# An input projection reordered: rows normalised first, gate tiles in pairs of seven chained products, attention last

## The chip, the cores and the metric

The kernel runs on one core of a Trainium2 chip. The metric is the device time of one launch in microseconds (us). The engines are named as in the profile: PE multiplies matrices (PEld loads its stationary operand), DVE is the vector engine, ACT the scalar engine, POOL the third elementwise engine, and SP issues the DMAs.

## The reference, cut to what matters

One encoder layer is applied to 512 prompt rows and 1024 sample rows (two sequences, same weights), with 1024 features, all in fp32:

```python
h = rms_norm(x, norm1_g)                       # per row
z = h @ w_in                                   # 1024 -> 6400 columns, 50 tiles of 128
#   conv value, conv gate (512) | pool (256) | short conv gb, gc, xv (768) | q, k, v (768) | gates (4 x 1024)
br_a = silu(layer_norm(depthwise31(a_val * sigmoid(a_gate)) + b)) @ w_out_a
br_b = pooled_means(z_pool) @ w_out_b
br_c = (gb * depthwise3(gc * xv)) @ w_out_c
br_d = neighbourhood_attention(q * 64**-0.5, k, v, rpb) @ w_out_d      # 4 heads of 64
merged = sum_i sigmoid(gate_i + b_i) * br_i
x = x + merged @ w_o
x = x + conv_glu_ffn(rms_norm(x, norm2_g))     # w_up 1024 -> 5632, depthwise3, silu, w_down 2816 -> 1024
return rms_norm(x, final_g)
```

## The kernel before

Everything is kept transposed: features on the 128 partitions, rows along the free axis, in three chunks of 512 rows (chunk 0 is the prompt, chunks 1 and 2 the sample). To keep fp32 accuracy each operand is split into a rounded high part and a low remainder, and each product is three matmuls (`mm3`, L112 to L115): high by high, high by low, low by high. One output tile of the input projection (128 of the 6400 columns) takes 3 chunks x 8 k-tiles x 3 = 72 matmuls of 512 columns. The order of the instructions on each engine is fixed at compile time by the framework's scheduler, which takes the earliest instruction of the program that it holds ready; on the chip each engine then works its queue in that order.

**Start.** The rows are split as they come, multiplied by the norm's gain alone (`split_x`, L109, L110). The two first gate tiles (PSUM tiles `zs`) follow the loads. The sums of squares are made beside them (`stats`), and the reciprocal root of the mean is broadcast to all partitions by a matmul with ones (`rms_scale`, `spread`) and kept in SBUF as `rb1`. Since the rows are not normalised, each tile that leaves PSUM is multiplied by `rb1` (`gate_evac`, L310).

**Plan.** The other 48 tiles stand in a list. After each tile `pump` emits background work up to a budget of 7.0:

```python
attention_pair(0); run_gates(9); drain()
conv_branch(0); run_gates(2); conv_branch(1); run_gates(9); drain()
then(conv_norm); attention_pair(1); run_gates(G3); drain()
pool_branch(0); run_gates(1); pool_branch(1); run_gates(1); drain()
short_branch(0); short_branch(1); run_gates(32)
```

An attention step (24 in all, a head pair by a block of 128 queries, cost 5.0) gathers its window of v on POOL (`vw`, L473), transposes it on PE (`vt`, L478) and splits it; then come scores, softmax, transposes of the probabilities (`tp`) and the product with v (`o`, L524 to L526). The 31 taps of each conv half run over 1552 columns on DVE (L579).

**Later stages.** A stage with eight PSUM tiles multiplies the branches by `w_out` (`y`), weighs them with the gates read back from DRAM and adds (`m`). Then `w_o` follows (`o`, L113 to L115), the second norm and the up projection. There 22 pairs of w_up tiles are each computed as two prompt tiles (24 matmuls each) and, for chunks 1 and 2, seven products of half-size blocks (12 matmuls each) in place of eight, in Winograd's form of Strassen's scheme. The sums of the weight blocks (`S1` to `S4`) are made on POOL, and the sums of the products on ACT and DVE. Last the down projection (`yp`) and the final norm.

Of the kernel before, what the change touches and what calls it, by code (L numbers as in the profile page):

```python
# [12 lines left out]
F32 = mybir.dt.float32  # L13
# [27 lines left out]
BUDGET = 7.0  # L41
# [3 lines left out]
SC_AT, EV_AT = 5, 15  # L45
ST = 3
G3 = 8
# [14 lines left out]
def encoder(ctx, tc, xT, w_in, w_out, w_o, w_up, w_dn, par, rrel, outT):  # L62
# [3 lines left out]
    def dram(name, shape):  # L66
        return tc.dram_tile(shape, F32, name=name)
# [8 lines left out]
    f_d = [dram(f"f_d{j}", [P, T]) for j in range(NJ)]  # L76
    late_d = {(n, k): dram(f"late_d{n}{k}", [P, C]) for n in LATE for k in range(4)}
# [34 lines left out]
    def mm3(ps, w, ws, x, first, last):  # L112
        PE.matmul(ps, w[0][:, ws], x[0], start=first, stop=False)  # L113
        PE.matmul(ps, w[0][:, ws], x[1], start=False, stop=False)  # L114
        PE.matmul(ps, w[1][:, ws], x[0], start=False, stop=last)  # L115
# [61 lines left out]
    with ExitStack() as outer:  # L177
# [42 lines left out]
        class UpWeights:  # L220
            def __init__(self):
                self.q = {}
# [5 lines left out]
            def parts(self, j):  # L228
                a = {}
                for n, f in (("1", NJ + j), ("2", j)):  # L230
                    raw = wp.tile([P, DM], F32, tag="wraw", name=f"wr_u{f}")
                    SP.dma_start(raw, w_up[f])
                    a[n + "1"], a[n + "2"] = raw[:, :C], raw[:, C:]
                w = self.q[j] = {}

                def plain(n):
                    w[n] = hl(f"A{n}h{j}"), hl(f"A{n}l{j}")
                    split(*w[n], a[n])

                def combo(n, tag, x, y, op):  # L240
                    t = self.stp.tile([P, C], F32, tag="st", name=f"S{n}_{j}")
                    G.tensor_tensor(t, x, y, op)
                    return t

                def mixed(n, tag, t):
                    o = wp.tile([P, DM], F32R, tag=tag, name=f"S{n}s{j}")
# [20 lines left out]
        wq = UpWeights()  # L267
# [10 lines left out]
        open_zps(4)  # L278

        def prompt(j, n):  # L280
            z = ztile(f"pp{n}{j}")
# [4 lines left out]
        def product(z, w, xn):  # L286
            for k in range(4):
                mm3(z, w, cols(k), ops[xn, k], k == 0, k == 3)
            return z

        with ExitStack() as mixer:
            bigp = pool(mixer, "bigp", 9)
# [7 lines left out]
            br = {}  # L300
            with ExitStack() as p1:
                sps = pool(p1, "sps1", 2, space=PSUM)
                mps = pool(p1, "mps1", 2, space=PSUM)
                gop = pool(p1, "gop", 3)
                rb1 = gop.tile([P, T], F32, tag="rb", name="rb1", bufs=1)

                def gate_evac(i, d):
                    def evac(c, z):
                        o = gop.tile([P, C], F32, tag="go", name=f"go{i}{d}{c}")
                        V.tensor_tensor(o, z, rb1[:, ch(c)], ALU.mult)  # L310
                        S.activation(o, o, AF.Sigmoid, bias=pc("bg", i * 8 + d))  # L311
                        SP.dma_start(gate_d[d][:, c, i, :], o)

                    return evac

                def gate_idx(i, d):
                    return 18 + 8 * i + d

                gates = [(i, d) for d in range(8) for i in range(4)]

                h = [[None] * KT for _ in range(NC)]
                with ExitStack() as p0:
                    np0 = pool(p0, "np0", 2)
                    xk = [big(f"x{k}") for k in range(KT)]
                    first = [load_w(w_in[gate_idx(*gates[n])], f"s{n}", None, (P, C)) for n in range(2)]

                    def load_x(k, c):
                        SP.dma_start(xk[k][:, ch(c)], xT[k * P : (k + 1) * P, ch(c)])

                    def split_x(k, c):  # L330
# [885 lines left out]
```

## Time and profile before

| | |
|---|---|
| time, median of 3 runs | 2269.69 us (2267.65 to 2270.16) |
| span of the profiled execution, first to last instruction | 2265.9 us |
| the three times stand above that span by | 1.8 to 4.3 us; the profiled execution's own time is not listed apart |
| PE busy | 2231.1 us, 9986 matmuls |
| DVE, ACT, POOL busy | 1339.6, 720.9, 545.9 us |
| moved by DMA | 195.63 MB |

Matmuls are pipelined: a recorded duration reaches over the start of the next, so the pace is read from start to start.

### The profile page before, as it was taken

What the parts mean: (1) busy time and instruction counts of PE and PEld (TensorE: products, weight loads), DVE (VectorE), ACT (ScalarE), POOL (GpSimd) and SP (SyncE); (2) the same over time, 40 slices, a digit from 0 to 9 for tenths busy, and PEclk for the clock granted to TensorE, in tenths of its full rate; (3) what the DMA queues carried; (4) which work ended last, traced back from release to release, by engine and by line L of the source; (5) the groups of instructions that cost most, each with busy time, mean ns of one, the idle gap of its engine ahead of it and who ended that gap; (6) DMA issues with size and microseconds to landing.
All of it is one profiled execution on the core that took longest, in us unless ns stands there. A gap on an engine that the chain in (4) does not pass through costs nothing.

```text
span 2265.9 us, 26328 instructions
## 1 busy us (share of the span) xinstructions
PE 2231.1 (98%) x9986; PEld 1817.6 (80%) x9986; DVE 1339.6 (59%) x1923; ACT 720.9 (32%) x1139; POOL 545.9 (24%) x671
## 2 busy tenths in 40 slices
PE   7999999999999999999998999999999999999997
PEld 5877888888777878888786788888888888888886
DVE  7345439932445442778339997777888876341414
ACT  6256411222156410302223543333333334221112
POOL 5023101000023101254234453344444430000001
PEclk9999999999999999999999999999999999999999
DMA  4211211222111110374432321111221225532231
GB/s 165 75 57 61 70 56 52 79 79 70 42 67 55 42 66 28 116 247 176 135 126 97 112 74 66 61 57 61 66 66 56 66 66 183 161 119 58 79 91 50
DMA packets 78351, 195.63 MB, mean 86 GB/s; under 512 B 8592, under 2 KB 11152, under 8 KB 75152
## 3 DMA queue, kind: packets, MB, share of 16 engines
q1 hardware_dynamic: 78224, 193.94, 25.6%
q8 instruction: 79, 1.29, 0.2%
q14 instruction: 48, 0.39, 0.1%
HBM read 135.71 MB, written 58.20 MB: 86 GB/s over the span
## 4 chain that ended last, share of the span: by engine, by line
PE 49%; DVE 2%; issue 0%; POOL 0%; ACT 0%; POOLq 0%; ACTq 0%
PE yp L113 5%; PE yp L114 5%; PE yp L115 5%; PE pp L114 3%; PE pp L115 3%; PE pp L113 3%; PE o L114 2%; PE o L113 2%; PE o L115 2%; PE p3T L115 1%; PE p3T L114 1%; PE p3T L113 1%; PE p1T L114 1%; PE p1T L115 1%; PE p1T L113 1%; PE p22T L115 1%
## 5 line engine op out<-in xcount | busy, mean ns | idle before, releaser
L113 PE MATMUL z<-hh,wh_i 128*128 128x512 f32 x1080 | 427.1, 395 | 0.0
L115 PE MATMUL z<-hh,wl_i 128*128 128x512 f32 x1080 | 423.6, 392 | 0.0
L114 PE MATMUL z<-hl,wh_i 128*128 128x512 f32 x1080 | 422.0, 391 | 0.0
L113 PEld LDWEIGHTS z<-hh,wh_i 128*128 128x128 f32 x1080 | 202.8, 188 | 46.4 <-issue 4.8
L115 PEld LDWEIGHTS z<-hh,wl_i 128*128 128x128 f32 x1080 | 202.8, 188 | 41.9 <-issue 0.7
L114 PEld LDWEIGHTS z<-hl,wh_i 128*128 128x128 f32 x1080 | 202.9, 188 | 40.9 <-issue 1.5
L113 PE MATMUL yp<-fs,wdhi 128*128 128x512 f32 x480 | 187.0, 391 | 0.0
L114 PE MATMUL yp<-fs,wdhi 128*128 128x512 f32 x480 | 186.9, 389 | 0.0
L115 PE MATMUL yp<-fs,wdlo 128*128 128x512 f32 x480 | 186.8, 389 | 0.0
L310 DVE TENSOR_TENSOR go<-z,rb 128x512 f32<-128x512 f32 x90 | 62.1, 690 | 193.2 <-PE z L115 193.2
L106 DVE TENSOR_TENSOR fs<-fr,fs 128x512 fp32r<-128x512 f32 x63 | 43.4, 691 | 182.1 <-ACT fs L105 182.1
L987 POOL TENSOR_TENSOR u<-u,u 128x512 f32<-128x512 f32 x63 | 97.6, 1549 | 193.5 <-DVE u L980 135.9
L311 ACT ACTIVATE go<-go,pt 128x512 f32<-128x512 f32 x96 | 69.4, 724 | 184.9 <-DVE go L310 180.0
L105 ACT CAST wh_i<-wr_i 128x1024 fp32r<-128x1024 f32 x44 | 46.3, 1052 | 241.9 <-PE z L114 224.4
L579 DVE SCALAR_TENSOR_TENSOR acc<-glu,pt,acc 128x1552 f32<-128x1552 f32 x60 | 112.7, 1879 | 1.6 <-ACT acc L577 0.4
L113 PEld LDWEIGHTS yp<-fs,wdhi 128*128 128x128 f32 x480 | 90.1, 188 | 19.3 <-issue 0.5
L114 PEld LDWEIGHTS yp<-fs,wdhi 128*128 128x128 f32 x480 | 90.1, 188 | 19.2 <-issue 0.5
L115 PEld LDWEIGHTS yp<-fs,wdlo 128*128 128x128 f32 x480 | 90.1, 188 | 18.9
L105 ACT CAST fs<-fr 128x512 fp32r<-128x512 f32 x63 | 39.1, 622 | 200.6 <-DMA fr<-f_d 98.7
L980 DVE SCALAR_TENSOR_TENSOR u<-c,pt,u 128x512 f32<-128x512 f32 x88 | 100.4, 1179 | 0.0
L1080 POOL TENSOR_TENSOR x<-x,rs 128x256 f32<-128x256 f32 x11 | 7.6, 731 | 366.1 <-DVE acc L1068 362.4
L979 DVE SCALAR_TENSOR_TENSOR u<-c,pt,u 128x512 f32<-128x512 f32 x88 | 86.9, 1025 | 0.0
(353 smaller groups left out, 4998.3 us busy)
## 6 DMA issues: line engine op xcount, KB each, us to landing
gate_d<-go SPq DMA_DIRECT2D x96, 256.0 KB, 2.0
g<-gate_d SPq DMA_DIRECT2D x24, 1024.0 KB, 4.9
wr_i<-in_w_in SPq DMA_DIRECT2D x45, 512.0 KB, 3.5
wr_u<-in_w_up SPq DMA_DIRECT2D x44, 512.0 KB, 3.5
f_d<-u SPq DMA_DIRECT2D x66, 256.0 KB, 2.0
fr<-f_d SPq DMA_DIRECT2D x66, 256.0 KB, 2.7
wdr<-in_w_dn SPq DMA_DIRECT2D x23, 512.0 KB, 3.7
x<-in_xT SPq DMA_DIRECT2D x24, 256.0 KB, 5.4
```

The costliest lines, as they stand in the source:

```text
L105: S.copy(hi, src)
L106: V.tensor_tensor(lo, src, hi.bitcast(F32), ALU.subtract)
L113: PE.matmul(ps, w[0][:, ws], x[0], start=first, stop=False)
L114: PE.matmul(ps, w[0][:, ws], x[1], start=False, stop=False)
L115: PE.matmul(ps, w[1][:, ws], x[0], start=False, stop=last)
L310: V.tensor_tensor(o, z, rb1[:, ch(c)], ALU.mult)
L311: S.activation(o, o, AF.Sigmoid, bias=pc("bg", i * 8 + d))
L579: V.scalar_tensor_tensor(a, g, w, a, ALU.mult, ALU.add)
L979: V.scalar_tensor_tensor(b, r[:, 0:C], pc("fc", f * 3), b, ALU.mult, ALU.add)
L980: V.scalar_tensor_tensor(b, r[:, 2 : C + 2], pc("fc", f * 3 + 2), b, ALU.mult, ALU.add)
L987: (V if j == NJ - 1 else G).tensor_tensor(uv, uv, ug, ALU.mult)
L1080: G.tensor_tensor(x, x, rs[:, :n], ALU.mult)
```

## The change

1. The rows of a chunk are normalised before they are split (`normalise`). So the first matmul needs the sum of squares over all eight k-tiles of chunk 0. No tile is multiplied by `rb1` on its way out. The first tiles are q0, q1 and k0 together.
2. q and k are written to DRAM in split form (`qk_d`). v is computed with the rows as stationary operand and 256 columns moving (`value_tile`), which gives it with rows on the partitions, and is written to DRAM once for each of four column blocks (`vt_d`). An attention step loads its v window in split form (`vv`); the gather, the transposes and the split of v are gone. The softmax's scaling by `ri` goes from DVE to ACT.
3. The two conv gates and values are computed early, their product is written to DRAM (`glu_d`), the taps run beside the gates in five steps per pair, and their result is written out as well (`acc_d`).
4. Thirty of the 32 gate tiles are computed as 15 pairs: the prompt chunk as before, chunks 1 and 2 by seven block products. Partial sums stay in PSUM: a product goes on adding to the tile of an earlier one after ACT or DVE has read it (`chain`).
5. Four normalised tiles that these pairs consume are read back and split again. Then a plan of 10 plain tiles follows (pool, short conv, two gates), with the 24 attention steps of cost 1.0 and a budget of 3.0 per tile, and the conv branch's layer norm beside the last two tiles.

```diff
-BUDGET = 7.0
+STEPS = 3.0
+TAPS = 5
+TPN = 34
-SC_AT, EV_AT = 5, 15
+SC_AT = 4
-G3 = 8
...
+    qk_d = {(n, p, x): dram(f"{n}{x}_d{p}", [P, T]) for n in "qk" for p in range(2) for x in "hl"}
+    vt_d = dram("vt_d", [4, T // GW, 32, 4 * P])
+    glu_d = [dram(f"glu_d{i}", [P, T]) for i in range(2)]
+    acc_d = [dram(f"acc_d{i}", [P, HI - LO]) for i in range(2)]
+    b12_d = [dram(f"b12_d{k}", [P, C]) for k in range(4)]
...
-        def product(z, w, xn):
+        def product(z, w, xn, first=True, chain=False):
             for k in range(4):
-                mm3(z, w, cols(k), ops[xn, k], k == 0, k == 3)
+                mm3(z, w, cols(k), ops[xn, k], first and k == 0, k == 3, chain)
             return z
...
+            def stats(c):
+                acc = tt(f"acc0_{c}")
+                for k in range(KT):
+                    if k == 0:
+                        S.activation(acc, x[k, c], AF.Square)
+                        continue
+                    q = tt(f"sq0_{c}{k}")
+                    S.activation(q, x[k, c], AF.Square)
+                    (G if c else V).tensor_tensor(acc, acc, q, ALU.add)
...
+            def normalise(k, c):
+                V.scalar_tensor_tensor(x[k, c], x[k, c], pc("g1", k), stat[c], ALU.mult, ALU.mult)
+                h[c][k] = hl(f"hh{k}_{c}"), hl(f"hl{k}_{c}")
+                split(*h[c][k], x[k, c])
+                if c == 2 and k < 4:
+                    SP.dma_start(b12_d[k], x[k, c])
...
+            stats(0)
+            scale(0)
+            for a in range(2):
+                split(*k0w[a], kraw[:, a * C : (a + 1) * C])
+            for c in range(NC):
+                zz = [ztile(f"zt{c}{n}") for n in range(3)]
+                if c + 1 < NC:
+                    stats(c + 1)
+                for k in range(KT):
+                    normalise(k, c)
+                    for n in range(3):
+                        w, ws = trio_w(n, k)
+                        mm3(zz[n], w, ws, h[c][k], k == 0, k == KT - 1)
+                    if k == SC_AT and c + 1 < NC:
+                        scale(c + 1)
+                for n in range(3):
+                    qk_out(*(("q", 0), ("q", 1), ("k", 0))[n], c, zz[n])
...
+            def value_tile(c, b):
+                z = ztile(f"zv{c}{b}")[:, :256]
+                for k in range(KT):
+                    xh, xl = (y[:, cols(b)] for y in h[c][k])
+                    wh, wl = (vw[m][k // 2][:, (k % 2) * 256 : (k % 2) * 256 + 256] for m in range(2))
+                    PE.matmul(z, xh, wh, start=(k == 0), stop=False)
+                    PE.matmul(z, xh, wl, start=False, stop=False)
+                    PE.matmul(z, xl, wh, start=False, stop=(k == KT - 1))
...
+            pairs = [(gates[2 * n], gates[2 * n + 1]) for n in range(15)]
+            wg = PairWeights("g", lambda n: tuple(w_in[gate_idx(*g)] for g in pairs[n]), tt)
+            wg.prepare(0)
+            for n, (ga, gb) in enumerate(pairs):
+                w = wg.q[n]
+                y, wz, xz = (ztile(f"{m}g{n}") for m in "ywx")
+                product(y, w["11"], "B11", True, True)
+                a = go(f"ga{n}")
+                S.copy(a, y)
+                if n + 1 < len(pairs):
+                    wg.prepare(n + 1)
+                z = prompt(n, "1", wg)
+                gate_out(*ga, 0, z, go(f"gp{n}"))
+                product(y, w["2"], "T2", False, True)
+                u2 = go(f"gu{n}")
+                S.copy(u2, y)
+                next(tap, None)
+                product(wz, w["3"], "T3", True, True)
+                p7 = go(f"gs{n}")
+                S.copy(p7, wz)
+                next(tap, None)
+                product(xz, w["12"], "B21")
+                V.tensor_tensor(a, xz, a, ALU.add)
+                gate_out(*ga, 1, a, a)
+                product(y, w["1"], "T1", False, True)
+                V.tensor_tensor(p7, y, p7, ALU.add)
+                gate_out(*gb, 2, p7, p7)
+                next(tap, None)
+                z = prompt(n, "2", wg)
+                gate_out(*gb, 0, z, go(f"gq{n}"))
+                next(tap, None)
+                product(wz, w["22"], "T4", False, True)
+                V.tensor_tensor(u2, wz, u2, ALU.add)
+                gate_out(*gb, 1, u2, u2)
+                product(y, w["4"], "B22", False, True)
+                gate_out(*ga, 2, y, go(f"gr{n}"))
...
-                        vw = ap.tile([P, 384], F32, tag="vw", name=f"vw{nm}", bufs=1)
...
-                        for i in range(nt):
-                            PE.transpose(vtp[:, cols(i)], vw[:, cols(i)], ident)
...
+                        vv = ap.tile([P, 3, 2 * P], F32R, tag="vv", name=f"vv{nm}")
+                        SP.dma_start(vv[:, :nt].bitcast(F32), vt_d[...])
...
-                            V.tensor_scalar(sv, sv, ri, None, ALU.mult)
+                            S.activation(sv, sv, AF.Copy, scale=ri)
...
                     def start():
-                        t["ot"] = br[3, p] = big(f"ot{p}")
+                        for n in "qk":
+                            for m in "hl":
+                                pl_, tag = (bigp, "big") if n == "q" else (kp, "k")
+                                t[n + m] = pl_.tile([P, PADW], F32R, tag=tag, name=f"{n}{m}{p}")
+                                SP.dma_start(t[n + m][:, :T].bitcast(F32), qk_d[n, p, m])
...
                 attention_pair(0)
-                run_gates(9)
+                pool_branch(0)
+                pool_branch(1)
+                sc = [short_head(0)]
                 drain()
...
+                attention_pair(1)
+                sc.append(short_head(1))
+                for g in gates[2 * len(pairs) :]:
+                    plain_gate(*g)
                 drain()
                 then(conv_norm)
+                for i in range(2):
+                    short_tail(i, sc[i])
                 drain()
```

## Rows read from the trace of the kernel before

**Rows 1.** The page: span, and busy time by engine.

```profile
span 2265.9 us, 26328 instructions
PE 2231.1 (98%) x9986; PEld 1817.6 (80%) x9986; DVE 1339.6 (59%) x1923; ACT 720.9 (32%) x1139; POOL 545.9 (24%) x671
```

**Rows 2.** PE's waits, longest first: total us, times, longest us.

```profile
PE rb L145 <- DVE dg L137: 5.7, 3, 2.7
PE zs L113 <- ACT hh L109: 5.3, 1, 5.3
```

**Rows 3.** Windows: start, 18 up-projection pairs, attention. Busy us (instructions) by engine.

```profile
0.00:60.00 60.00, 47.06 (x181) 33.46 (x182) 48.07 (x63) 37.95 (x62) 32.56 (x25) 0.97 0.45 160
1270.31:1810.67 540.36, 540.36 (x2378) 446.05 (x2377) 448.96 (x538) 204.19 (x333) 239.91 (x354) 1.00 0.19 63
10.00:20.00 10.00, 8.17 (x30) 5.44 (x29) 9.65 (x8) 9.62 (x18) 8.41 (x6) 1.00 1.05 397
```

**Rows 4.** PE in order of time: first matmuls, plain tile, attention.

```profile
7.10 0.63 PE L113 MATMUL zs<-hh,wh_s 128*128 128x512 f32 x1
7.53 0.63 PE L114 MATMUL zs<-hl,wh_s 128*128 128x512 f32 x1
...
208.74 0.28 PE L526 MATMUL o<-ph,vl 128*128 128x256 f32 x1
...
209.45 0.28 PE L526 MATMUL o<-ph,vl 128*128 128x256 f32 x1
...
215.72 0.49 PE L478 MATMUL vt<-pt,vw 128*128 128x128 f32 x3
216.15 0.45 PE L489 MATMUL s<-kh,qh 64*128 64x384 f32 x2
...
216.88 0.50 PE L113 MATMUL z<-hh,wh_i 128*128 128x512 f32 x1
...
224.15 0.44 PE L489 MATMUL s<-kh,qh 64*128 64x384 f32 x1
```

**Rows 5.** Groups by line and shape: count, busy us, mean ns of one.

```profile
L525 PEld LDWEIGHTS o<-pl,vh 128*128 128x128 f32 x64 | 12.1, 188 | 3.2 <-issue 1.3 <-DVE pl L106 1.2
L110 DVE SCALAR_TENSOR_TENSOR hl<-x,pg,hh 128x512 fp32r<-128x512 f32 x24 | 30.0, 1286 | 5.8 <-ACT hh L109 5.8
L856 DVE SCALAR_TENSOR_TENSOR x<-x,pg,rb 128x512 f32<-128x512 f32 x16 | 10.9, 740 | 0.3 <-PE rb L145 0.3
L992 ACT COPY a<-p11B 128x512 f32<-128x512 f32 x20 | 11.3, 567 | 0.0
L371 ACT ACTIVATE sq<-x 128x512 f32<-128x512 f32 x21 | 13.1, 623 | 3.7 <-POOL acc L372 3.6
L579 DVE SCALAR_TENSOR_TENSOR acc<-glu,pt,acc 128x1552 f32<-128x1552 f32 x60 | 112.7, 1879 | 1.6 <-ACT acc L577 0.4
```

**Rows 6.** DVE and PE in order of time: one reciprocal root and its broadcast.

```profile
2015.40 0.94 PE L132 MATMUL rb<-ones,acc 128*128 128x1 f32 x8
...
2016.38 0.16 DVE L135 TENSOR_SCALAR rs_v<-rb 128x4 f32<-128x4 f32 x1 [2.21 <-PE rb L132]
...
2018.55 0.69 DVE L137 TENSOR_TENSOR acc<-pt,rs_y 128x512 f32<-128x512 f32 x1
...
2019.30 1.13 PE L145 MATMUL rb<-acc,ones 128*128 128x512 f32 x2
```

**Rows 7.** SP and ACT at the start: a load's issue, its reader.

```profile
1.66 0.42 SPq L328 DMA_DIRECT2D x<-in_xT  x1
...
4.53 0.72 ACT L109 ACTIVATE hh<-x,pg 128x512 fp32r<-128x512 f32 x1 [1.07 <-DMA x<-in_xT]
```

**Rows 8.** ACT in order of time within one attention step.

```profile
217.89 1.28 ACT L511 ACT_TABLE_LOAD   x1
...
222.79 0.99 ACT L105 CAST ph<-tp 128x384 fp32r<-128x384 f32 x2 [1.97 <-PE tp L517]
```

**Rows 9.** DMA issues: count, KB each, median us from issue to landing.

```profile
g<-gate_d SPq DMA_DIRECT2D x24, 1024.0 KB, 4.9
```

## What the change does to the time, forecast from these rows

> **What bounds the kernel now.** I read the page first. PE is busy for 2231 of 2266 us [rows 1], but a matmul's record overlaps the next, so that alone proves little. The list of PE's waits is the test: its longest entries are 5.7 and 5.3 us in total, both around the first and second norm [rows 2]. PE therefore sets the end nearly everywhere, and a removed matmul is worth its start-to-start pace. That pace comes from a long undisturbed stretch: 2378 matmuls in 540.36 us [rows 3], 0.227 us each for 512 columns. Two other paces matter. The 256-column matmuls of the attention product start 0.12 us apart (six intervals from 208.74 to 209.45) [rows 4]. The three transposes of v take PE from 215.72 to 216.15, 0.143 us each [rows 4].
>
> The exception is the start. In the first 60 us there are 181 matmuls [rows 3], 24 of them one column wide (three roots of eight). The other 157 at 0.227 us need 35.6 us. The one-column ones and two broadcasts (0.94 us for eight, 1.13 us each [rows 6]) need about 5 us more. So close to 20 us of PE time is lost there.
>
> **The gate pairs.** Two plain tiles are 144 matmuls. A pair is two prompt tiles of 24 and seven products of 12, together 132. Fifteen pairs save 180 matmuls: 180 x 0.227 = **-40.9 us**. The up projection already runs such pairs, and there 18 pairs fill 540.36 us with PE at 100% while DVE is busy 448.96 us, 24.9 us a pair [rows 3]. What is new here is hidden in the same way. POOL makes the same four sums. DVE has the same eight remainders, three additions, and five taps of 1.88 us [rows 5], 9.4 us, in place of the up projection's own convolutions; I see no more than 25 us in a 30 us pair.
>
> What is not in the trace is the chain: a product adds to a tile that ACT or DVE has just read, so PE has to wait for that read. There are four such reads in a pair (the tile y three times, wz once). The copy is 0.57 us [rows 5]. Between product and continuation stand at least 24 matmuls of other tiles, 5.4 us. I cost the waits at nothing; if the cover is gone, each read exposes the copy and two handoffs, about 0.8 us, 4 x 15 x 0.8 = 48 us.
>
> **v.** Tiles 16 and 17 go: 144 x 0.227 = 32.7 us. In their place stand 12 x 24 = 288 matmuls of 256 columns: 288 x 0.12 = 34.6 us, **+1.9 us**. Each has a weight load of its own, recorded at 0.188 us [rows 5], longer than the matmul's pace. In the rows of the attention product the load of the same shape hides all the same, so I take 0.12. The bounds are half the 512-column pace (32.7 us, no change) and a pace of 0.188 (54.1 us, +21.5).
>
> The 64 transposes of v go: 64 x 0.143 = **-9.2 us**. At the 0.12 pace of the neighbouring matmuls it would be -7.7. The POOL gather, one copy and one subtract per step go with them. They were beside PE's work and count nothing. The same holds for the multiplication of each tile by `rb1`.
>
> Each value tile issues eight stores on SP, at 0.42 us each as at the start [rows 7] 3.4 us, against 2.9 us of PE work. SP falls some 6 us behind over twelve tiles, and the weights of the next tile (k1) may stand behind the stores in its queue. Bounds: nothing and +8. I take **+1**, since those weights can be asked for as soon as the raw buffer is free, long before.
>
> **The start.** Before, PE began when one k-tile had come. Now it needs all eight and their root. A load issued at 1.66 is used at 4.53, 2.9 us later [rows 7]. Eight loads are 2.1 MB, 5.3 us at the 397 GB/s of the stretch from 10 to 20 us [rows 3], so the last is there at about 9.0 us. Then one square (0.62 [rows 5]), one addition (0.69), the root's matmuls (0.94), the DVE chain to the end of the diagonal (2016.38 to 2019.24, 2.86), the broadcast (1.13) [rows 6], the normalisation (0.74 [rows 5]) and the cast of the high part (0.62): 7.6 us, with handoffs PE starts at about 17.3 us. The first matmuls also come at half pace. At 7.10 and 7.53 they are 0.43 us apart [rows 4], the lower level of the clock; about twelve at that level cost 2.4 us. The first remainder adds 0.7 us.
>
> After that a k-tile gives PE nine matmuls, 2.04 us, and DVE a normalisation and a subtraction. The subtraction of two SBUF operands took 1.29 us on average while POOL added squares [rows 5], so DVE needs 2.03 us: a tie. I allow 1.5 us for it. Loss about 22 us, against 20 before: **+2 us**. Bounds: -3 if the rows arrive earlier, and +13 if the root of chunks 1 and 2 (6.3 us from its first matmul to the first cast, by the same rows) is late at each of the two borders. What covers it is the preceding chunk, 72 matmuls or 16.3 us: POOL's seven additions and the root fit if the loads have come by 20 us.
>
> **Attention at the end.** Ten plain tiles (10 x 72 x 0.227 = 163 us) now cover 24 steps. A step costs PE 0.73 us for scores (216.15 to 216.88 [rows 4]), 0.86 for six transposes at 0.143 and 1.08 for nine products, 2.7 us; 24 of them 64 us. The stage has 228 us of PE work. The chain through the steps must not be longer. Scores of one step to scores of the next took 8.0 us before (216.15 to 224.15 [rows 4]), with a table load of 1.28 us in the way [rows 8], which the sigmoids between them caused. Only two gate tiles are left here, so I expect 6.7. Then 24 x 6.7 = 161 us, plus the loads of q and k: 3.1 MB a pair, 8 us at 397 GB/s and 2.9 us of latency, 22 us for both pairs. Behind them the layer norm has three roots of 5 us. Sum 198 us, below 228. At 8.0 us a step it is 229, a tie. The products of the other three branches (nine of six matmuls, 12 us) can go ahead at the seam. I take **+3** between nothing and +13 (9 us a step: 253 less 228 and 12).
>
> The reload of four normalised tiles lies behind 48 matmuls of chunks 0 and 1, 10.9 us; four loads (1 MB, 4.9 us in the nearest row [rows 9]) and four splits of 1.3 us just fit.
>
> **Sum.** -40.9 + 1.9 - 9.2 + 1 + 2 + 3 = -42.2 us. The profiled span of 2265.9 becomes 2223.7. The median of the runs stands 3.8 us above that span, which I carry over: **2227.5 us**.
>
> **Rivals.**
> *The weight load shows in the value tiles.* At the load's pace of 0.188 us they cost 19.6 us more than I took: 2247. Against it speaks that six equal intervals of 0.12 us hold loads of just this shape. Chance 0.03. In its strict form each load waits for the matmul before it: 288 x 0.188 = 54 us more, 2281.6, slower than before. Chance 0.01.
> The Trainium skill, page "TensorE: Matmul & The Clock Gate", section "The mechanism" under packing small matmuls, states this strict form: a weight load overlaps matmuls in flight only if it goes to other row groups. This case's trace does not agree: the loads take all 128 rows and the matmuls still start 0.12 us apart [rows 4, 5].
>
> *The border roots are late.* Two of 6.3 us at the start: 2240. For it speaks that POOL shares the time with DVE there (1.29 against 0.74 us). Chance 0.07.
>
> *Attention becomes the bound (the other side).* From 8.5 us a step the chain (24 x 8.5 + 37 = 241) passes the 240 us of cover, and each further microsecond costs 24. At 10.2 us a step the gain is gone. At 11 us the chain is 301 us, 61 over the cover: 2227.5 - 3 + 61 = 2285.5. For it: three steps follow each other per tile, each waits for its own v load, ACT has one more operation in the chain, and DVE's pool sums now fall into this stage. Against it: 8.0 us was reached with table loads. Chance 0.11, of which 0.05 lies beyond 10.2.
>
> *The chained reads are exposed.* All four: 2227.5 + 48 = 2275.5. It decides against the change from 42.2 / 15 = 2.8 us a pair. That needs ACT to be 5 us behind in nearly every read, and the up projection's ACT, at 204.19 us in 540, was not. Chance 0.05, of which 0.03 slower.
>
> **How the numbers follow.** The forecast with its bounds (2217 to 2240) has 0.73. The range 2217 to 2250 holds it, late roots, the milder load and a mild attention tail, and leaves out 0.06 below and about 0.13 above. Slower by over 0.2% (about what a measurement of this kernel can tell): 0.05 + 0.03 + 0.01 = 0.09. Within 0.2%, from a tail or exposed reads that just eat the gain: 0.03. Faster: 0.88.
>
> **What would show it.** Gate pairs: 30.0 us per 132 matmuls with PE at 100%; gaps ahead of the matmuls of y and wz, released by ACT copies, would prove me wrong. Value tiles: 24 matmuls in 2.9 us. First matmul at 17.3 us, some 22 us lost by 60. No PE wait of more than a few us where the last plain tile meets the first branch products. 180 + 64 + 144 matmuls fewer and 288 more, 9886 in all. The prediction fails if PE waits over 20 us in the last stage of the projection or at the start.

## The result, and the profile after

The changed kernel takes 2298.3 us (2297.95 to 2299.61, four runs) against 2269.1 us in the same comparison: ratio 1.0130, interval 1.0116 to 1.0144. It is 29 us slower. The forecast was 2227.5 us, 42 us faster, so it missed by 71 us and in sign.

The page of the kernel after, to be laid beside [rows 1]: span, then busy time by engine.

```profile
span 2296.3 us, 26705 instructions
PE 2206.6 (96%) x9886; PEld 1792.0 (78%) x9886; DVE 1331.7 (58%) x1928; ACT 768.3 (33%) x1306; POOL 623.1 (27%) x690
```

PE does the work that was forecast, 9886 matmuls, and is busy 24 us less, in a span that is 30 us longer. So the loss is waiting. PE's waits in the kernel after, total us, times, longest us; [rows 2] began at 5.7:

```profile
PE rb L140 <- DVE acc L350: 20.6, 1, 20.6
PE rb L153 <- DVE dg L145: 11.4, 4, 6.2
PE tp L635 <- ACT se L632: 6.1, 9, 1.3
PE y L121 <- ACT bh L112: 4.6, 1, 4.6
PE y L122 <- DVE bl L113: 4.5, 6, 1.0
PE rbl L153 <- DVE dgl L145: 4.3, 1, 4.3
PE yg L121 <- ACT ga L503: 4.3, 3, 3.0
...
PE yg L121 <- ACT gu L510: 3.4, 1, 3.4
PE zt L122 <- DVE hl L113: 2.5, 2, 1.5
PE yg L121 <- DVE gs L520: 2.4, 1, 2.4
PE zt L121 <- ACT hh L112: 2.3, 1, 2.3
```

Four places stand in it: the start (`rb`, `zt`), the gate pairs (`yg`), attention (`tp`) and the seam between projection and branch products (`rbl`, `y`). Windows of the kernel after, columns as in [rows 3]: the start, the first 150 us of the pairs (four and a half of them), later pairs, and the seam.

```profile
0.00:60.00 60.00, 26.66 (x103) 19.88 (x103) 33.88 (x63) 25.59 (x45) 19.96 (x21) 1.00 0.47 169
211.00:361.00 150.00, 139.86 (x585) 113.27 (x584) 134.22 (x101) 45.28 (x77) 42.79 (x23) 0.95 0.28 97
360.00:660.00 300.00, 300.00 (x1325) 248.40 (x1324) 72.69 (x109) 106.95 (x171) 52.80 (x38) 1.00 0.30 94
917.00:960.00 43.00, 32.81 (x131) 22.38 (x130) 20.58 (x57) 12.09 (x15) 3.85 (x3) 0.88 0.18 62
```

The later pairs run as forecast, PE at 100% and 0.226 us a matmul; the first 150 us hold 585 matmuls where 662 would fit, at a mean granted clock of 0.95. From start to start of all records of both executions, with 0.227 us for 512 columns, 0.12 for 256 and 0.11 for 128 (the interval between two transposes), the ledger is as follows; an entry shifts by 1 us or so (those of the seam and the tiles ahead of it by up to 3) with the pace taken for the few other shapes and with where a border is drawn:

| stage | PE lost before, us | after | difference | forecast |
|---|---|---|---|---|
| start, to the first value tile (93.4 us after, first 50 us before) | 21.1 | 39.3 | +18.2 | +2 |
| value, q, k, conv tiles, to 211 us | - | 1.8 | +1.8 | +1 |
| fifteen pairs, 211 to 678 us | - | 17.7 | +17.7 | 0 |
| other tiles of the projection, attention among them | 14.8 | 28.2 | +13.4 | 0 |
| seam and branch products | 2.1 | 25.2 | +23.1 | +3 |
| all that follows | 25.6 | 27.6 | +2.0 | 0 |
| PE's own work (324 matmuls of 512 columns and 64 transposes fewer, 288 of 256 more) | | | -46.0 | -48.2 |

The differences add up to +30.2; the spans differ by 30.4 us.

The start, kernel after, in order of time, several engines:

```profile
11.54 1.06 ACT L116 ACTIVATE wh_q<-wr_q 128x1024 fp32r<-128x1024 f32 x1 [9.52 <-DMA wr_q<-in_w_in]
12.63 2.53 DVE L117 SCALAR_TENSOR_TENSOR wl_q<-wr_q,wh_q 128x1024 fp32r<-128x1024 f32 x2 [11.63 <-ACT wh_q L116]
...
13.80 0.61 ACT L346 ACTIVATE acc<-x 128x512 f32<-128x512 f32 x1
...
15.07 5.46 DVE L350 TENSOR_TENSOR acc<-acc,sq 128x512 f32<-128x512 f32 x7
...
20.59 1.86 PE L140 MATMUL rb<-ones,acc 128*128 128x1 f32 x8 [20.59 <-DVE acc L350]
22.13 0.33 SPq L339 DMA_DIRECT2D pt<-in_par  x1
...
27.93 0.69 DVE L145 TENSOR_TENSOR dg<-pt,rs_y 128x512 f32<-128x512 f32 x1 [1.22 <-DMA pt<-in_par]
...
28.68 2.08 PE L153 MATMUL rb<-dg,ones 128*128 128x512 f32 x2 [6.23 <-DVE dg L145]
...
30.79 3.38 DVE L360 SCALAR_TENSOR_TENSOR x<-x,pg,rb 128x512 f32<-128x512 f32 x5 [0.96 <-PE rb L153]
...
33.02 0.79 PE L121 MATMUL zt<-hh,wh_q 128*128 128x512 f32 x1 [2.27 <-ACT hh L112]
```

The rows are there early, but ACT stands in front of the q weights until 11.54, with the squares behind them; the sum follows the remainders of those weights; the diagonal waits 1.22 us for the identity in `pt`, which is asked for at 22.13, behind the rows of all chunks. The root's small matmuls and its broadcast take 1.86 and 2.08 us, against 0.94 and 1.13 [rows 6]. The first product comes at 33.0 us.

A chained read in the pairs, kernel after:

```profile
225.35 7.36 DVE L490 SCALAR_TENSOR_TENSOR acc<-glu,pt,acc 128x1552 f32<-128x1552 f32 x3
...
228.41 2.67 POOL L250 TENSOR_TENSOR Sg<-Sg,wr_g 128x512 f32<-128x512 f32 x1
...
231.11 0.62 ACT L112 CAST Sg2s<-Sg 128x512 fp32r<-128x512 f32 x1 [5.89 <-POOL Sg L250]
231.64 0.58 ACT L510 COPY gu<-yg 128x512 f32<-128x512 f32 x1
...
232.27 0.50 PE L121 MATMUL yg<-T1h,Sg1s 128*128 128x512 f32 x1 [3.42 <-ACT gu L510]
```

It reads backwards: PE may not go on adding to `yg` until ACT has copied it; ACT's copy stands in the queue behind the cast of a weight sum; that waits for POOL, whose addition takes 2.67 us beside DVE's taps. (In e2 below, where no tap stands beside them yet, the same pair's four additions take 1.29 us each and end 10.3 us after the first began; here it is 14.6.) After the wait the granted clock is 0.54 from 233.0 to 236.5 us, the lower of its two levels (1.2 and 2.4 GHz) for most of it, with records 0.43 us apart.

Not every late read goes by POOL. The second longest wait, kernel after:

```profile
286.48 0.72 ACT L308 ACTIVATE gu<-gu,pt 128x512 f32<-128x512 f32 x1 [4.57 <-DVE gu L527]
...
288.20 0.57 ACT L503 COPY ga<-yg 128x512 f32<-128x512 f32 x1
...
288.83 0.79 PE L121 MATMUL yg<-T2h,Sg2s 128*128 128x512 f32 x1 [2.99 <-ACT ga L503]
```

Here ACT stands 4.57 us in front of an addition of DVE's that comes late behind taps, and the copy stands behind it. The 2.4 us on `gs` are a read of DVE's own, behind taps in its queue.

The seam, kernel after:

```profile
947.23 0.95 PE L140 MATMUL rbl<-ones,lsq 128*128 128x1 f32 x8
...
952.46 2.08 PE L153 MATMUL rbl<-dgl,ones 128*128 128x512 f32 x2 [4.29 <-DVE dgl L145]
954.57 1.28 DVE L705 TENSOR_TENSOR accn<-accn,rbl 128x512 f32<-128x512 f32 x2 [2.17 <-PE rbl L153]
...
955.30 3.25 ACT L710 ACTIVATE accn<-accn,pt 128x1552 f32<-128x1552 f32 x2 [6.62 <-DVE accn L705]
958.46 1.12 ACT L112 CAST bh<-accn 128x512 fp32r<-128x512 f32 x2
...
959.11 0.80 PE L121 MATMUL y<-bh,wh_wo 128*128 128x512 f32 x1 [4.57 <-ACT bh L112]
959.48 1.14 ACT L112 CAST bh<-ob 128x512 fp32r<-128x512 f32 x2
```

The last attention product is at 916.9 us, the last plain tile ends at 946. The third root of the layer norm follows both; silu follows the root, and the casts of all four branches follow silu on ACT.

### The profile page after: what moved, and what is told of

It reads as the page before. It is cut to its first block, busy times and chain, and to the rows that moved or that the text cites. A ratio compares the mean times of both kernels' runs of the same rounds, so it can differ in the third digit from the quotient of the medians.

```text
span 2296.3 us, 26705 instructions
## 1 busy us (share of the span) xinstructions
PE 2206.6 (96%) x9886; PEld 1792.0 (78%) x9886; DVE 1331.7 (58%) x1928; ACT 768.3 (33%) x1306; POOL 623.1 (27%) x690
## 4 chain that ended last, share of the span: by engine, by line
PE 48%; DVE 3%; issue 0%; POOL 0%; ACT 0%; POOLq 0%; DVEq 0%; ACTq 0%
PE yp L122 5%; PE yp L123 5%; PE yp L121 5%; PE ppu L122 3%; PE ppu L123 3%; PE ppu L121 3%; PE o L122 2%; PE o L121 2%; PE o L123 2%; PE p3T L122 1%; PE p3T L121 1%; PE p3T L123 1%; PE p1T L122 1%; PE p1T L123 1%; PE p1T L121 1%; PE p4B L123 1%
## 5 line engine op out<-in xcount | busy, mean ns | idle before, releaser
L490 DVE SCALAR_TENSOR_TENSOR acc<-glu,pt,acc 128x1552 f32<-128x1552 f32 x60 | 122.7, 2044 | 9.3 <-ACT acc L488 8.4
L123 PEld LDWEIGHTS yp<-fs,wdlo 128*128 128x128 f32 x480 | 90.1, 188 | 18.7
L616 POOL TENSOR_TENSOR bm<-R,pt 128x384 f32<-128x384 f32 (+1 forms) x48 | 52.7, 1104 | 149.0 <-DVE mx L623 123.3
L121 PE MATMUL z<-hh,wh_i 128*128 128x512 f32 x200 | 82.1, 410 | 0.0
L250 POOL TENSOR_TENSOR Sg<-wr_g,wr_g 128x512 f32<-128x512 f32 x15 | 22.6, 1504 | 219.2 <-DVE Sg1s L113 219.2
L122 PE MATMUL y<-bl,wh_wo 128*128 128x512 f32 x192 | 77.1, 402 | 4.8 <-DVE bl L113 4.5
L123 PE MATMUL z<-hh,wl_i 128*128 128x512 f32 x200 | 81.5, 408 | 0.0
L122 PE MATMUL z<-hl,wh_i 128*128 128x512 f32 x200 | 80.2, 401 | 0.0
L121 PE MATMUL y<-bh,wh_wo 128*128 128x512 f32 x192 | 74.8, 395 | 4.6 <-ACT bh L112 4.6
L1060 ACT ACTIVATE u<-u 128x512 f32<-128x512 f32 x66 | 41.8, 633 | 110.3 <-DVE u L1054 110.2
L122 PE MATMUL o<-ml,wh_o 128*128 128x512 f32 x192 | 75.5, 393 | 1.2 <-DVE ml L113 1.2
```

The lines of the kernel that those rows point to most:

```text
L121: PE.matmul(ps, w[0][:, ws], x[0], start=first, stop=False, **kw)
L122: PE.matmul(ps, w[0][:, ws], x[1], start=False, stop=False, **kw)
L123: PE.matmul(ps, w[1][:, ws], x[0], start=False, stop=last, **kw)
L490: V.scalar_tensor_tensor(a, g, w, a, ALU.mult, ALU.add)
L616: G.tensor_tensor(bmv, rv, cm[:, None, :].broadcast_to([P, nk, 32]), ALU.add)
L1060: S.activation(ug, ug, AF.Silu)
```

## The experiments

Times are medians beside runs of the kernel before (2268 to 2269 us each time); "after" is 2298.3 us.

**e1, e2: the taps.** In e1 the sixty taps on DVE are gone; in e2 they stay, five a pair, each held in DVE's queue behind one of the pair's own additions.

```diff
+            def hold(ins, n):
+                with tc.issue_after(ins.ins):
+                    for _ in range(n):
+                        next(tap, None)
-                V.tensor_tensor(a, xz, a, ALU.add)
+                hold(V.tensor_tensor(a, xz, a, ALU.add), 2)   # likewise 1 behind p7, 2 behind u2
```

> The changed kernel with 60 of the 62 conv taps on DVE left out (only the first tap of each half, on ACT, is made), so the conv branch's values are not the reference's. Theory: of the changed kernel's excess, about 17 us arise between 211 and 360 us, where the taps stand in rows on DVE, hold POOL's weight sums back, and so the ACT casts and the copies of the chained tiles queued behind these casts; without taps the five PE waits there (10.1 us together, and the low clock after them) vanish and the time is 15 to 18 us less, about 2281. Rival: the chained reads are late by themselves, whatever DVE does; then the waits of the yg tiles stay and the time falls by less than 3 us.

> The same sums as the changed kernel; the five taps of a pair are queued on DVE behind that pair's own additions, so that they spread over 13 pairs in place of five and a half. Theory (bunched taps): the waits of the yg tiles between 211 and 360 us shrink to under 3 us in total and the time falls by 12 to 18 us, to about 2283. Rival (chained reads late by themselves): the waits stay or spread over more pairs, time within 3 us of 2298.

Measured: 2280.8 us (1.0050, 1.0031 to 1.0070) and 2281.2 us (1.0050, 1.0030 to 1.0069), 17.5 and 17.1 us less than after. Window of e2, the same 150 us:

```profile
211.00:361.00 150.00, 150.00 (x664) 124.20 (x663) 81.99 (x80) 52.95 (x86) 37.23 (x22) 1.00 0.27 86
```

PE is at 100% and DVE is busy 82 us in place of 134. The taps need not go; they must not come ten a pair. Within the noise these are the 17.7 us of the pairs: 10.1 us of waits on `yg`, and most of the rest the lower clock behind them (0.95 over 150 us is some 7 us, an estimate from the window).

**e6: no pairs.** Thirty plain tiles in the same place, two or three taps beside each; the four normalised tiles are not read back.

```diff
-            for n, (ga, gb) in enumerate(pairs):
-                ...
+            for n, g in enumerate(gates[:30]):
+                for c, z in tile_of(f"g{n}", gw.next()):
+                    gate_out(*g, c, z, go(f"go{n}{c}"))
+                for _ in range(2 + n % 2):
+                    next(tap, None)
```

> The thirty gate tiles are computed in the same place as plain tiles of 72 matmuls, with two or three taps beside each; the four normalised tiles are not read back. Everything else is as changed. It tells what the pairs are worth by themselves. PE has 180 matmuls more, 40.9 us at 0.227. Theory (the 17.7 us lost while the taps run come from pairs and taps together: chained reads stand behind tap-locked POOL sums): plain tiles have no chained read and no POOL sums, so they lose next to nothing beside the same taps, and the time is 2298 + 41 - 17 = 2322 us. Rival (taps delay any gate tile, since DVE also empties its PSUM tiles): 2336 to 2340 us, with PE waits on the PSUM tiles of the plain tiles.

Measured: 2324.4 us (1.0246, 1.0232 to 1.0260), as the theory has it. The pairs are worth 26 us as they stand, some 15 short of their 41, and the taps cost e6 next to nothing: its plain tiles have no chained read, and POOL no weight sums to make.

**e3, e9, e12: the start.** e3 asks for the identity right behind chunk 0, makes the statistics of chunk 0 ahead of the q weights, and the statistics of a later chunk after the second k-tile of the one before.

```diff
+            SP.dma_start(pt, par[:, NG:])
+            stats(0); scale(0)
             trio = [load_w(w_in[12], "q0", HD**-0.5), load_w(w_in[13], "q1", HD**-0.5)]
...
+                    if k == 1 and c + 1 < NC:
+                        stats(c + 1)
```

> Same sums; program order at the start alone: the table with the identity is loaded right after the eight loads of chunk 0, the squares and the root of chunk 0 stand before the casts of the q weights, and the squares of chunk 1 behind the second k-tile. Theory: the first matmul of the projection came at 33.0 us because ACT made two weight casts (11.5 to 13.9 us) before the first square, the diagonal waited for the identity's load, and three squares of chunk 1 stood before the first cast; it now comes at 20 to 24 us, and the time falls by 8 to 12 us. Rival: the loads of chunk 0 themselves are late; then the first matmul stays beyond 28 us and the time falls by under 4 us.

Measured: 2291.8 us (1.0099, 1.0070 to 1.0129), 6.5 us less where 8 to 12 were expected. These are two runs, and the interval overlaps that of the kernel after; the trace is clearer. In the eight traces whose start is as changed the first value tile comes at 92.0 to 96.4 us (93.4 in the kernel after), in e3 at 88.1. The first product comes at 23.6 us in place of 33.0, so part of the gain is given back at the borders between chunks. e9 lets the rows be split without the root, which is still computed:

```diff
-                V.scalar_tensor_tensor(x[k, c], x[k, c], pc("g1", k), stat[c], ALU.mult, ALU.mult)
+                V.tensor_scalar(x[k, c], x[k, c], pc("g1", k), None, ALU.mult)
```

> The rows of the first norm are multiplied by the gain alone, so the first products need no sum of squares and no root; the sums, the three roots and their broadcasts are still computed, and their result is left unused. It tells what waiting for the root costs at the start, all else as changed. Theory (most of the 18 us lost there come from the dependency: PE can begin once one k-tile and the q weights are split, and nothing waits at the two borders): first projection matmul at 15 to 18 us instead of 33, 14 to 18 us faster, about 2282 us. Rival (the casts of the q weights and the order of the vector queues set it, the root only lies beside them): first matmul not before 25 us, at most 8 us faster, 2290 us.

Measured: 2297.0 us (1.0123, 1.0107 to 1.0138), 1.3 us less, which cannot be told from nothing: the intervals overlap. Neither theory has it so. PE's waits of e9 in the first 95 us:

```profile
PE rb L140 <- DVE acc L350: 22.2, 1, 22.2
PE rb L153 <- DVE dg L145: 5.1, 1, 5.1
PE rb L140 <- POOL acc L350: 3.1, 1, 3.1
```

The products no longer need the sum, but the root's small matmuls stand ahead of them in PE's queue and do: the first product is at 24.0 us. What is gained goes back at the borders, where PE stands at the next roots. e12 leaves out squares, sums, roots and broadcasts too (`stats` and `scale` are not called):

> The squares, sums, roots and broadcasts of the first norm are left out altogether and the rows are multiplied by the gain alone; all else as changed. When the products merely no longer used the root (they still came behind its matmuls in PE's queue), the first of them came 9 us earlier but 7 of these were given back at the two borders, where PE waited 3.1 us for POOL's sums and 5.1 us for the third root. Theory (the statistics themselves fill DVE, ACT and POOL at the start and hold PE's fixed queue at each root): without them the first product starts at about 15 us, no wait at the borders is left, 5.4 us of PE's own work for roots and broadcasts go, and the time is 20 to 24 us less, 2276 us. Rival (the start is set by the loads of the rows and by splitting them and the weights): 8 to 12 us less, 2288 us.

Measured: 2273.3 us (1.0020, 1.0011 to 1.0030), 25 us less. PE's waits of e12 in the first 95 us:

```profile
PE zt L121 <- ACT wh_q L116: 12.8, 1, 12.8
PE zt L123 <- DVE wl_q L117: 0.6, 1, 0.6
PE zt L121 <- ACT k0h L112: 0.5, 1, 0.5
```

The first value tile is at 66.2 us in place of 93.4. So loads and splits hold the first product until 12.8 us and no longer; the rest of the start is the statistics. Some 5.4 us of the 25 are PE's own matmuls for them. e12 takes away their work together with their place in the queues, so how much the place alone costs it does not say.

**e4, e5: the layer norm.** e4 leaves it out, silu with it. e5 does it beside the last gate pairs and reads the finished branch back:

```diff
+                for c in range(NC):
+                    for fn in (center, scale_c, apply):      # in the generator of the taps
+                        fn(c)
+                        yield
+                for i in range(2):
+                    S.activation(b, b, AF.Silu, bias=pc("lb", i), scale=pc("lg", i))   # b: rows LO to HI of half i
+                    SP.dma_start(br0_d[i], b)
```

> The layer norm and silu of the conv branch are left out (its taps' result goes on as it is), so the output is not the reference's. Theory: the layer norm that begins when the last attention step is done holds back the splits of all branches, and PE stands 24 us between 920 and 985 us; without it the products with the branch weights follow the last plain tile as before the change and the time falls by 20 to 27 us (the norm's own PE work, about 5 us, included), to about 2274. Rival: the stall comes from attention's tail or the reload of the gates; then the seam keeps over 12 us of waiting and the time falls by 5 to 8 us.

> The layer norm and silu of the conv branch are done beside the last gate pairs, and their result, not the bare accumulator, is written out and read back. Theory (at the seam the branch products wait because the norm's chain of roots starts only when attention is done, and the splits of the other three branches queue behind the silu): without the norm at all the time fell by 34 us, about 10 of them PE's own work for the norm; here that work stays and the 24 us of waiting go, so 2274 us (2271 to 2279), and no PE wait on lsq, dgl or bl between the last plain tile and y. Rival (the wait at the seam is for the attention's own last results, and the norm only hides it): the first y matmul follows the last plain tile as late as before, less some us for the norm's own matmuls, 2288 us or more. Rival (the norm's DVE and ACT work delays the chained reads of the pairs that it now runs beside): the pairs after 360 us no longer run at 30.0 us, and 5 to 10 us come back, 2280 to 2285 us.

Measured: 2263.9 us (0.9977, 0.9966 to 0.9988) and 2276.5 us (1.0035, 1.0021 to 1.0049): 34.4 and 21.8 us less. e4 gains more than the 20 to 27 that were expected, since the norm's own 42 matmuls on PE, some 10 us, went with it. PE's waits of e5 from 600 to 1100 us:

```profile
PE tp L675 <- ACT se L672: 6.1, 9, 1.2
PE o L123 <- DVE ml L114: 1.2, 1, 1.2
PE rbl L154 <- DVE dgl L146: 0.9, 1, 0.9
```

No wait of `y` is left. The seam's loss was the norm's late place, nearly all of it.

**e7, e10: the softmax's scaling.** e7 puts it back on DVE, e10 leaves it out.

```diff
-                            S.activation(sv, sv, AF.Copy, scale=ri)
+                            V.tensor_scalar(sv, sv, ri, None, ALU.mult)      # e7; e10: no line
```

> The softmax's scaling goes back from ACT to DVE; all else as changed. Theory (ACT's extra operation lengthens the chain of an attention step; PE waits 6.1 us for it in nine steps, and the pace from a plain tile to the transposes of the probabilities is 0.43 us on average against 0.27 before the change): 3 to 6 us faster, 2293 us, and PE's waits on the scaled probabilities under 3 us. Rival (the chain is set by the load of v or by the exponential, and DVE has the pool sums in this stage): no change within 2 us, the waits move to DVE's result.

> The softmax's division by its sum is left out altogether (48 operations on ACT); all else as changed. Putting it back on DVE made the kernel 8 us slower, so the scaling is on the chain of a step and the engine that does it matters. Theory (PE stands in front of the transposes because its fixed order puts them earlier than the scaled probabilities are there): without the scaling PE's waits of 6.1 us in nine steps go and the stage loses 6 to 8 us less, 2291 us. Rival (the transposes then wait for the exponential instead, or the switches between shapes are what costs): less than 3 us.

Measured: e7 2306.5 us (1.0166, 1.0151 to 1.0182), 8.2 us more where 3 to 6 less were expected; e10 2293.5 us (1.0108, 1.0095 to 1.0122), 4.8 us less, though its interval just overlaps that of the kernel after. Two of e7's waits from 600 to 1100 us:

```profile
PE tp L635 <- DVE se L632: 9.3, 13, 2.0
...
PE tp L635 <- DVE ri L631: 3.7, 5, 1.8
```

The theory for e7 fell: ACT is the better place here. That DVE also makes the pool sums in this stage may be why; it was not tested. e10 lies between its two theories: the transposes then wait 3.3 us for the exponential, in seven steps. By the intervals between records, from a plain tile to a transpose PE lost 1.8 us before, 9.5 after, 7.8 in e10 and 18.2 in e7.

**e8: three edits together**, held taps, early statistics, early norm.

> Three edits together: taps held behind the pair's additions, the statistics of the first chunk ahead of the casts of the q weights, the layer norm beside the last pairs. If the three losses are separate places on PE's path, as the theory has it, the gains add up: -17.1 - 6.5 - 24 = -48 us, 2251 us, faster than the kernel before the change (2269) by 0.8%. If they share a cause or the held taps run so late that the early norm then comes too late and waits, the sum falls short: 2265 to 2275 us.

Measured: 2251.7 us (0.9931, 0.9918 to 0.9943), faster than the kernel before by 16.5 us. The gains add up: 17.1 + 6.5 + 21.8 = 45.4, measured 46.6. Against the forecast 24 us are still missing: some 11 in the start (15.4 us to PE's first record and 18.7 lost behind it, 34 in all where 21 before and the forecast's +2 make 23), 2 in the transposes of v, and most of the rest around the attention steps.

**e11, e13, e14: the start of e8.** e11 gives PE small matmuls to do ahead of the first root; e13 fewer of them, and the rows of chunk 1 earlier; e14 also asks for the sums of chunk 1 ahead of the casts.

```diff
+            def spin(n):
+                for _ in range(n):
+                    PE.matmul(wm[:, :P], ones, ones, start=True, stop=True)
             stats(0)
+            spin(52)      # e11: 90; 12 (20) more ahead of the broadcast, 7 (8) behind it
...
+            for k in range(KT):
+                load_x(k, 1)      # e13, e14: ahead of the weights of k
+            stats(1)              # e14
```

> The version with three edits (taps held, statistics first, layer norm beside the last pairs; 2251.7 us) plus 118 small matmuls of ones by ones, whose result nobody uses, ahead of the first root, between root and broadcast and behind it. In that version PE's records up to 28.2 us are 0.43 us apart, at half the pace, and the root's eight small matmuls and its broadcast take 1.86 and 2.07 us against 0.94 and 1.13 at full pace. Theory (the granted clock is low because PE had nothing to do until 15.4 us): with PE kept busy the first 12 or so matmuls, the root and the broadcast run at full pace, 2.4 + 0.9 + 0.9 = 4 us, 2247.5 us. Rival (the clock falls again in the gaps that stay, or the small matmuls come into the way of the root): within 2 us of 2251.7, or slower by their last 1 to 2 us.

> The version with three edits (2251.7 us) with 71 small matmuls of ones by ones in place of the 118 that ended 7 us too late (each took 0.22 us at full pace, two records), and with the rows of chunk 1 loaded ahead of the weights of k, so that their sums can begin some 7 us earlier. Theory (clock and border wait are separate losses): the small matmuls end at about 14.4 us, the root is not delayed, the first products run at full pace (about 4 us), and the border wait for POOL's sum (3.2 us) goes: 2245 us. Rival (POOL's earlier sums now run beside the chain of the first root on DVE and stretch it): 2250 us, with the diagonal ready later than the 19.3 to 20.0 us of before.

> The version with the small matmuls and the early rows of chunk 1 (2254.7 us; its first product came 1.7 us earlier than in the version with three edits, at full pace, but the border then waited 4.1 us for POOL's sum of chunk 1, which began only at 31.8 us, since the squares of chunk 1 stood on ACT behind the casts of chunk 0) with those squares and sums asked for ahead of the casts, in the time in which ACT stands idle for the first root (14.2 to 21.4 us). Theory (POOL's sum of chunk 1 is what is late next): the border wait of 4.1 us and most of the 2.0 us for the second diagonal go, 2248 us. Rival (POOL's sum now runs beside the chain of the first root on DVE and stretches it, and the second border is late instead): no change within 2 us of 2252 to 2255.

Measured: 2261.6 us (0.9966, 0.9953 to 0.9978), 2254.7 (0.9939, 0.9927 to 0.9952) and 2250.2 (0.9919, 0.9906 to 0.9933). PE of e11 in order of time:

```profile
1.05 21.96 PE L357 MATMUL warm<-ones 128*128 128x128 f32 x180 [1.05 <-DVE ones L95]
22.85 0.95 PE L141 MATMUL rb<-ones,acc 128*128 128x1 f32 x8
...
28.21 1.02 PE L154 MATMUL rb<-dg,ones 128*128 128x512 f32 x2
```

e11 is 10 us slower than e8, outside both of its theories. Their clock part held, broadcast at 1.02 us in place of 2.07 and the first products at 0.23; but the small matmuls stood in front of the root, which came at 22.85 us in place of 15.4. In e13, which changes two things at once, they ended in time, the first product came at 22.0 us in place of 23.7, and the first value tile was no earlier (88.5 and 88.2): the border then waited 4.1 us for POOL's sum of chunk 1, and the time cannot be told from e8's. e14 took that wait away and shows the rival's contention, though in DVE's splits and not in the root's chain. DVE and POOL of e14:

```profile
24.10 0.69 DVE L114 TENSOR_TENSOR hl<-x,hh 128x512 fp32r<-128x512 f32 x1
...
24.71 12.84 POOL L344 TENSOR_TENSOR acc<-acc,sq 128x512 f32<-128x512 f32 x8 [23.78 <-ACT sq L343]
...
28.45 7.97 DVE L114 TENSOR_TENSOR hl<-x,hh 128x512 fp32r<-128x512 f32 x5
```

A remainder takes 0.69 us alone and 1.6 beside POOL's sum. The first value tile is at 85.6 us, and this time cannot be told from e8's either: the intervals overlap.

## Why the prediction was wrong, by its steps

**PE's work was nearly right.** 9886 matmuls; 288 value matmuls from 93.44 to 128.0 us, 34.6 us as forecast, with a load of 0.188 us for each, so the rival of the visible load came true in neither form. The term of the transposes was 2 us too large: the 0.143 us taken for each holds the switch to the scores behind them, and two transposes follow each other at 0.11. The pairs run at their pace once the taps are done.

**The gate pairs: "five taps of 1.88 us", "no more than 25 us in a 30 us pair".** This step failed. On average it holds: a later pair has 7.3 us of DVE work, and five taps would add 9.4. But the sixty taps began between 187.3 and 353.8 us, more than ten a pair: the program asks for five, but the queue's order came from what the scheduler held ready, and nothing held a tap back. DVE was busy 134 of 150 us. The rival of the exposed chained reads, given 0.05, came true in part: 17.7 us and not 48, since five of the sixty reads were late and it ended with the taps. Its condition (ACT behind in its queue) was right for four of the five; its cause, taps bunched on DVE, which slow POOL and hold DVE's own additions, was not in it. e1 and e2 show that cause, e6 that plain tiles beside taps do not suffer.

**The start: "17.3 us", "+2".** The term was +18. The sum laid squares, sum and root end to end behind the last load and left out what stands between them in the queues: two weight casts on ACT, their remainders on DVE, and a load for the identity behind 24 loads of rows. By the same sum the first product is 15.7 us late: the sum of squares was done at 20.5 us where the terms give 10.3; DVE's chain to the diagonal took 6.1 us in place of 2.86, two of its small steps 1.11 us in place of 0.16 while POOL added squares, and 1.22 the wait for the identity; and the root's matmuls and the broadcast took 1.9 us more at half pace, which the sum had reckoned for the products alone. Its first step, that PE begins when the root is there, was too simple as well: e9 shows that PE's queue waits for each root even where no product needs it. The rival of late roots (0.07, +12.6) was the nearest. Earlier statistics and an earlier identity, moved together, give back 6.5 us (e3; 5.3 by the first value tile). e12 bounds the rest; how much of it a better order could save was not settled: e13 and e14 each removed one wait and met the next.

**Attention at the end: "the chain through the steps must not be longer", "+3".** Attention did not become the bound: its last product is 29 us ahead of the last plain tile's end. Two things were missed. The forecast priced the norm's three roots as length inside the cover, but their place is at its end, and "The products of the other three branches ... can go ahead at the seam" was false: their casts stand behind silu in ACT's queue. That is +23.1, of which e5 gives back 21.8. And the steps cost PE 13.4 us more around them: 7.7 of it from plain tiles to the transposes, which wait for the probabilities. Leaving out the scaling gives back 4.8 in all (e10), but only 1.7 in this place, so most of it stays open. The rest was only read from the intervals, not tested: 33 switches from the product `o` to scores in place of 17, at 0.13 us each, some 2 us; and 3.8 us between the score matmuls of 384 columns, of which 24 in 65 started within 0.01 us of the one ahead before the change and 6 in 66 after it.

## What to carry to other kernels

Price a moved step by where it lands in each engine's fixed queue, not by the engine's average load: two of the three large misses were operations that had time enough and stood behind something that had not, and the third was work that nobody had told to wait. Cover counts only if the order spends it evenly; work given to an engine "beside" something needs an edge that keeps it there. A wait removed at a start is worth what the next wait leaves of it.

## What was not expected of the hardware

DVE and POOL slow each other, both ways: between 211 and 361 us POOL's addition took 2.17 us beside the taps (median of 20, up to 2.88) against 1.29 in e1 without them, a tap up to 2.87 us against 1.83, and in e14 DVE's remainder 1.6 us beside POOL's sum against 0.69. The Trainium skill, page "SBUF — State Buffer", section "Who interferes with whom", says that a DVE instruction with two SBUF inputs contends with a GpSimd instruction that reads SBUF; the trace agrees, and in the wait at 232 us what it cost was PE's time, two engines further on.

A PE that had done next to nothing until 33 us began its products at 0.43 us a matmul, the pace of the lower clock level, although the profile's clock column says 1.00 there. The trace has no record of the clock before 38.7 us, where the intervals fall to 0.23, so at a start the level is read from the intervals. In e11 small matmuls that nobody uses, from 1 us on, brought the first products to 0.23. It saved nothing that could be measured: in e11 they delayed the root, and in e13 a sum on POOL was the next to be late.
